# The second expert stage of a two-layer block: rows gathered and scattered by DMA in place of products on TensorE

## The chip, the cores and the metric

The kernel runs on one core of one Trainium2 chip. The metric is the device time of one execution in microseconds (us). A core has TensorE (PE, with its weight loads shown as PEld), VectorE (DVE), ScalarE (ACT), GpSimd (POOL) and SyncE (SP), which run side by side, each in its own order, and 16 DMA engines that all queues share.

## The reference

A two-layer block over 256 latent and 256 context tokens of 1024 numbers, in fp32. Each layer has a mixer and then a mixture of experts. The second layer's experts see only the 256 latent tokens:

```python
def moe(h, router_w, router_bias, w_gate, w_up, w_down):
    t = h.reshape(-1, D_MODEL)
    score = jax.nn.sigmoid((t @ router_w).astype(jnp.float32))
    ...
    _, idx = lax.top_k(masked, TOP_K)          # TOP_K = 2 of N_EXPERTS = 16
    w = jnp.take_along_axis(score, idx, -1)
    w = w / jnp.sum(w, -1, keepdims=True)
    combine = jnp.sum(jax.nn.one_hot(idx, N_EXPERTS, dtype=jnp.float32) * w[..., None], 1).astype(t.dtype)
    out = jnp.zeros_like(t)
    for e in range(N_EXPERTS):
        hid = jax.nn.silu(t @ w_gate[e]) * (t @ w_up[e])   # 1024 -> 512
        out = out + combine[:, e:e + 1] * (hid @ w_down[e])  # 512 -> 1024
    return out.reshape(shp)
```

## The kernel before

**Weights.** Each expert has 6.3 MB of weights: two tiles of 1 MB (128 x 2048) each for gate, up and down. `Feeder.load` issues them on SP into a ring of tiles named `raw` and `rawx` (RAWA = 3 and, in the second stage, RAWB1 = 4). A tile is used in two halves. `Feeder.one` turns a half into a pair of tiles `hl` or `hlx`: ACT copies it rounded to the short fp32 format (line 138), and DVE or POOL subtracts that from the source for the low part (line 140). This is a *split*; an expert needs 12. POOL takes every third where `feed.pool_lo` is 3 (line 1557), otherwise DVE takes all. A pair is free again when PE has used it; there are 4 pairs, and HLX_1 more in the second stage.

**First stage** (`moe`, 512 tokens). For each expert a list of up to 128 tokens is made by comparing positions (`slots`, line 1128). `gather` (line 1141) fetches their rows from XN in DRAM with an indirect DMA on POOL; `xT` (line 1157) turns them on PE and splits them into high and low. `expert` runs the gate product, half of the next expert's up product, the turn of the hidden tile, the other half, and the down product, with one split behind each block of products; every product is three matmuls (high by high, high by low, low by high). The result, times its weight, goes to YD in DRAM with an indirect DMA (line 1149). YD has a row for either of a token's two experts; at the end it is read back and summed. The last two experts don't go through DRAM: their rows are added by products with a 0/1 matrix (line 1349).

**Second stage** (`moe_latent`, 256 tokens). The experts are sorted by how many tokens they have; the places in BIG (0, 1, 4, 9) hold up to 128 tokens, the other twelve up to 64. Two small ones share an operand tile ("unit"), and high and low parts stand side by side in its 128 columns, so that a product has two matmuls of 512 columns instead of three (line 1553; 864 in all). Rows are not gathered. `collect` (line 1433) multiplies `xn`, which stays in SBUF, by the 0/1 matrix `PG` (line 1424), 16 matmuls in fp32 for each half of a unit's operand. A small expert's halves are added by products with `fold` (lines 1609, 1613). The result `y` is split into high and low (lines 1648, 1649) and added into four PSUM banks that are held through the stage: `combine`, eight matmuls an expert (line 1538) with the 0/1 matrix `PT` (line 1635).

`overflow` is a branch for the case that an expert has more tokens than its place holds; here it is not taken. In the second stage it stands ahead of the last expert, and all engines pass it.

What sets the order: inside `in_order()` every engine runs its instructions in the order in which the code issues them, so an instruction that waits holds up those behind it on its engine.

Of the kernel before, what the change touches and what calls it, by code (L numbers as in the profile page):

```python
# [56 lines left out]
HLX_1, AHEAD_1 = 4, 6  # L57
# [111 lines left out]
def _body(tc, nc, pool, psum, dram, a):  # L169
# [677 lines left out]
    def normed(layer, r, nh):  # L847
# [7 lines left out]
        for i in range(2):  # L855
            t = x_ = xn[:, D * i + 512 * nh:D * i + 512 * nh + 512]
            if layer:

                t = tmp()
                x_ = xn[:, D * i:D * i + D].rearrange("q (k p) -> q p k", k=8)[:, 64 * nh:64 * nh + 64]  # L860
            V.scalar_tensor_tensor(t, Hh(2 * r + i, nh), rs[:, 2 * r + i:2 * r + i + 1], psc, OP.mult, OP.mult)
            b_ = sh if engs[i] == "G" else psh
            if layer:
                t, b_ = (w.rearrange("q (p k) -> q p k", k=8) for w in (t, b_))
            XENG[engs[i]].tensor_tensor(x_, t, b_, OP.add)
# [111 lines left out]
    YD = dram.tile([1024, D], F32, name="YD")  # L977
    rank = pool.tile([128, 4, NE], F32, name="rank")
# [31 lines left out]
    def overflow(layer, nt, pl, pos, prepare=None, expert=None, finish=None):  # L1010
# [3 lines left out]
        with tc.If(rv > 128):  # L1014
            if layer:
# [3 lines left out]
                prepare(y)  # L1019
# [9 lines left out]
            with tc.For_i(0, NE, 1) as e:  # L1029
                re = nc.values_load(cnti[0:1, bass.ds(e, 1)], min_val=0, max_val=top)  # L1030
                we = expert(e) if expert else e
                for q in range(1, nt if layer == 0 else nt + 1):
                    with tc.If(re > 128 * q):
# [14 lines left out]
                        for k in range(8):  # L1048
                            T.transpose(b_[2 + k // 4][:, 128 * (k % 4):128 * (k % 4) + 128], xg[:, 128 * k:128 * k + 128] if layer else xg[:, k::8], ident)
# [20 lines left out]
                        for nh in range(2):  # L1070
                            V.tensor_scalar(y[:, 512 * nh:512 * nh + 512], b_[nh], odisp[:, 2:3], None, OP.mult)
                        G.indirect_dma_start(out=YD, out_offset=bass.IndirectOffsetOnAxis(ap=odispi[:, 0:1], axis=0),
                                             in_=y, in_offset=None, bounds_check=256 * nt - 1, oob_is_err=False)
            if finish:
                finish([wt, xh])

    def route(layer, nt):
# [36 lines left out]
        V.tensor_copy(RM[:, :n_, :, 0], rk)  # L1114
# [4 lines left out]
    def moe(layer, nt, pl, before_tail=None):  # L1119
# [82 lines left out]
        overflow(layer, nt, pl, posm)  # L1202
# [175 lines left out]
    def moe_latent(pl, xn):  # L1378
# [11 lines left out]
        units.sort()  # L1390
        iota2 = pl.tile([128, 128], F32, name="iota2")
# [5 lines left out]
        for j in range(NE):  # L1397
            G.memset(rcol[:, j:j + 1], float(at[j]))
        kc = pl.tile([128, NE], F32, name="kc")
# [3 lines left out]
        RMS = pl.tile([128, 2, NE, 2], F32, name="RMS")  # L1403
        toffs = pl.tile([128, 2], F32, name="toffs")
        for i in range(2):
            G.tensor_scalar(RMS[:, i, :, 0], pcol[:, 0:1].broadcast_to([128, NE]), 128.0 * i + 1.0, None, OP.add)
            G.memset(toffs[:, i:i + 1], -128.0 * i - 1.0)
        wd = pl.tile([128, NE, 2], F32, name="wd")
        dcol = pl.tile([128, NE, 2], F32, name="dcol")
# [4 lines left out]
        perm = pl.tile([128, NE, NE], F32, name="perm")  # L1414

        xsteps, se, sc, mk, rk = route(layer, nt)
        xsteps(2)
# [9 lines left out]

        def collect(unit, PG, k4):

            pt = bank()  # L1430
            for k in range(4):
                for i in range(2):
                    T.matmul(pt[:, 128 * k:128 * k + 128], xn[:, D * i + 128 * (4 * k4 + k):D * i + 128 * (4 * k4 + k) + 128],
                             PG[:, i, 0] if len(unit) == 1 else PG[:, i, :, 0:64], start=i == 0, stop=i == 1)
            return pt

        def split_operand(unit, pt, s, k4):
            if len(unit) == 1:
# [518 lines left out]
```

## Time and profile before

| | |
|---|---|
| median of 3 runs | 1244.71 us (1241.48 to 1245.55) |
| the profiled execution | 1236.13 us, span 1234.4 us |
| PE, DVE, ACT, POOL busy | 88%, 72%, 59%, 32% of the span |
| mean granted clock of TensorE | 0.961 |
| DMA | 308 MB, mean 250 GB/s |
| first stage, from first to last expert's first product | 303.4 to 606.9 us |
| second stage, the same | 856.4 to 1200.0 us |

Shares of the whole span mix mixers and expert stages. The two stages are to be read apart, each by its stretch of the trace. Busy time of an engine counts what overlaps once. Times in the trace count from the start of the span.

### The profile page before, as it was taken

How to read it: one execution, taken by the hardware profiler on the slowest of the kernel's cores; microseconds unless marked ns; L12 is line 12 of the kernel's file. 1: busy time of each engine (PE TensorE's matmuls, PEld its weight loads, DVE VectorE, ACT ScalarE, POOL GpSimd, SP SyncE). 2: the span in 40 equal slices, each digit the busy share in tenths (PEclk: the TensorE clock that was granted, in tenths of full speed). 3: DMA queues.
4: the chain of work that ended last, by engine and by line, in shares of the span. 5: the costliest groups of instructions: out<-in, count | busy, mean ns of one | idle time of the engine just before them, and what ended most of it. 6: DMA issues, size and time to landing. Idle time of an engine off the chain costs nothing. (4 is left out here: it accounts for less than half of the span.)

```text
span 1234.4 us, 15863 instructions
## 1 busy us (share of the span) xinstructions
PE 1091.7 (88%) x5595; PEld 812.2 (66%) x5596; DVE 884.6 (72%) x1118; ACT 724.8 (59%) x973; POOL 389.4 (32%) x396
## 2 busy tenths in 40 slices
PE   5889999994999999998779999996699898998883
PEld 3546454783777778777467766675577777777662
DVE  3444561747889998898974345857989889789983
ACT  3326642434878888887534234533667677677771
POOL 3150561623011111111434100122435554544551
PEclk9999999997999999999979999998899998998997
DMA  9763666904899999997963778352678787879840
GB/s 301 219 192 115 202 189 225 360 30 149 333 373 350 359 349 363 377 351 271 337 199 80 255 242 303 137 238 69 239 256 299 267 304 281 317 263 326 280 152 34
DMA packets 96529, 308.15 MB, mean 250 GB/s; under 512 B 16494, under 2 KB 57601, under 8 KB 67256
## 3 DMA queue, kind: packets, MB, share of 16 engines
q1 hardware_dynamic: 89576, 293.38, 67.2%
q0 software_dynamic: 6864, 13.66, 3.5%
q8 instruction: 47, 0.77, 0.3%
q14 instruction: 42, 0.34, 0.1%
HBM read 299.15 MB, written 11.60 MB: 252 GB/s over the span
## 5 line engine op out<-in xcount | busy, mean ns | idle before, releaser
L140 DVE TENSOR_TENSOR hl<-raw,hl 128x1024 fp32r<-128x1024 f32 x126 | 168.4, 1353 | 116.4 <-ACT hl L138 92.7
L140 DVE TENSOR_TENSOR hl<-rawx,hl 128x1024 fp32r<-128x1024 f32 x167 | 226.3, 1382 | 29.3 <-ACT hl L138 23.0
L138 ACT ACTIVATE hl<-raw 128x1024 fp32r<-128x1024 f32 x140 | 145.7, 1055 | 119.9 <-PE psa L456 40.6
L138 ACT ACTIVATE hl<-rawx 128x1024 fp32r<-128x1024 f32 x178 | 185.5, 1060 | 44.4 <-PE psb L1169 12.6
L1169 PE MATMUL psb<-hl,xT 128*128 128x512 f32 x696 | 172.1, 400 | 0.0
L1169 PEld LDWEIGHTS psb<-hl,xT 128*128 128x128 f32 x696 | 127.7, 188 | 27.4
L1553 PE MATMUL psa<-hl,xT 128*128 128x512 f32 x432 | 116.6, 417 | 15.8 <-DVE xT L1633 15.0
L1553 PE MATMUL psa<-hlx,xT 128*128 128x512 f32 x432 | 114.8, 412 | 16.0 <-DVE xT L1633 12.3
L1553 PEld LDWEIGHTS psa<-hl,xT 128*128 128x128 f32 x432 | 84.4, 200 | 39.4 <-DVE xT L1633 13.0
L1553 PEld LDWEIGHTS psa<-hlx,xT 128*128 128x128 f32 x432 | 83.0, 197 | 38.3 <-DVE xT L1633 11.2
L1266 PE MATMUL psa<-hl,xT 128*128 128x512 f32 x192 | 77.6, 404 | 3.7 <-DVE hl L140 1.7
L1266 PE MATMUL psb<-hl,xT 128*128 128x512 f32 x192 | 77.3, 403 | 0.1
L456 PE MATMUL psa<-nT,hl 128*128 128x512 f32 x264 | 69.6, 408 | 4.7 <-POOL nT L490 2.5
L456 PEld LDWEIGHTS psa<-nT,hl 128*128 128x128 f32 x264 | 48.6, 189 | 28.6 <-issue 6.9
L1141 POOL DMA_INDIRECT xg<-XN,dispi x16 | 21.5, 1341 | 141.9 <-PE psa L1251 68.7
L140 DVE TENSOR_TENSOR hlx<-rawx,hlx 128x1024 fp32r<-128x1024 f32 x38 | 60.2, 1594 | 3.7 <-ACT hlx L138 3.7
L456 PE MATMUL psb<-nT,hl 128*128 128x512 f32 x216 | 58.1, 415 | 4.8 <-DVE hl L140 2.6
L140 POOL TENSOR_TENSOR hlx<-rawx,hlx 128x1024 fp32r<-128x1024 f32 x18 | 48.3, 2686 | 42.4 <-ACT hlx L138 36.5
L140 POOL TENSOR_TENSOR hl<-rawx,hl 128x1024 fp32r<-128x1024 f32 x17 | 46.4, 2728 | 40.8 <-ACT hl L138 34.0
L138 ACT ACTIVATE hlx<-rawx 128x1024 fp32r<-128x1024 f32 x54 | 55.5, 1055 | 4.9 <-PE psa L1553 4.8
L140 POOL TENSOR_TENSOR hl<-raw,hl 128x1024 fp32r<-128x1024 f32 x14 | 38.3, 2738 | 60.6 <-ACT hl L138 54.7
L456 PEld LDWEIGHTS psb<-nT,hl 128*128 128x128 f32 x216 | 41.5, 196 | 20.0 <-issue 4.2
(504 smaller groups left out, 2146.9 us busy)
## 6 DMA issues: line engine op xcount, KB each, us to landing
rawx<-in_moe_w_up_dram SPq DMA_DIRECT2D x41, 1024.0 KB
rawx<-in_moe_w_gate_dram SPq DMA_DIRECT2D x40, 1024.0 KB
rawx<-in_moe_w_down_dram SPq DMA_DIRECT2D x37, 1024.0 KB
raw<-in_ada_w_dram SPq DMA_DIRECT2D x32, 1024.0 KB
raw<-in_moe_w_down_dram SPq DMA_DIRECT2D x25, 1024.0 KB
raw<-in_moe_w_gate_dram SPq DMA_DIRECT2D x21, 1024.0 KB
raw<-in_moe_w_up_dram SPq DMA_DIRECT2D x20, 1024.0 KB
rawx<-in_ada_w_dram SPq DMA_DIRECT2D x16, 1024.0 KB
```

The costliest lines, as they stand in the source:

```text
L138: nc.scalar.activation(h3, src, AF.Copy, scale=1.0 if self.gate is None else self.gate)
L140: (nc.gpsimd if self.pool_lo and self.ns % self.pool_lo == 0 else nc.vector).tensor_tensor(l3, src, h3.bitcast(F32), OP.subtract)
L456: ins = T.matmul(pt, l, r, start=k == 0 and m == 0, stop=k == 7 and m == 2)
L1141: G.indirect_dma_start(out=xgs[e % 2], out_offset=None, in_=XN, in_offset=bass.IndirectOffsetOnAxis(ap=dispi[:, e, 1:2], axis=0), bounds_c ...
L1169: ins = T.matmul(out_, l, r_, start=m == 0, stop=m == last)
L1266: T.matmul(pb, l, w_[:, 512 * nh:512 * nh + 512], start=m == 0, stop=m == 11)
L1553: ins = T.matmul(po, l, w_[:, c0:c0 + 512], start=k == 0 and m == 0, stop=k == n * per - 1 and m == len(mm) - 1)
```

## The change

The second stage gets the first's ways and order. `gather` fetches a unit's rows from XN with an indirect DMA, `tokens` turns and splits them; `scatter` writes an expert's rows to a new DRAM tensor YL, 1024 rows of 1024 numbers: four for each token, two for either of its experts. A small expert writes both, from the high and the low columns of its tile; a big one writes the first alone, and the second rows are zeroed in the mixer. YL is read back ahead of the last expert and summed on POOL and DVE. `expert` has one split behind each block. All splits run on DVE (`pool_lo` stays 0). HLX_1 goes from 4 to 2.

```diff
-HLX_1, AHEAD_1 = 4, 6
+HLX_1, AHEAD_1 = 2, 6
...
-                x_ = xn[:, D * i:D * i + D].rearrange("q (k p) -> q p k", k=8)[:, 64 * nh:64 * nh + 64]
...
-        if nh and layer == 0:
+        if nh:
             for i in range(2):
                 Q.dma_start(XN[128 * (2 * r + i):128 * (2 * r + i) + 128], xn[:, D * i:D * i + D])
...
+    YL = dram.tile([1024, D], F32, name="YL")
...
-            PG = pl.tile([128, 512], F32, name="PG", tag="PG", bufs=2)[:, :256 * n].rearrange("p (i k s) -> p i k s", i=2, k=n)
+            PG = pl.tile([128, 512], BF, name="PG", tag="PG", bufs=3)[:, :256 * n].rearrange("p (i k s) -> p i k s", i=2, k=n)
...
+        def gather(n):
+            unit, PG = units[n], PGs[n]
+            pd = bank()
+            w = 128 // len(unit)
+            for c in range(len(unit)):
                 for i in range(2):
+                    for x_ in (2, 3):
+                        T.matmul(pd[w * c:w * c + w, 0:1], PG[:, i, c, :w], RM[:, i, unit[0], x_:x_ + 1],
+                                 start=i == 0 and x_ == 2, stop=i == 1 and x_ == 3)
+            V.tensor_scalar(gidx[:, n:n + 1], pd[:, 0:1], 4096.0, None, OP.add)
+            G.indirect_dma_start(out=xgs[n % 2], out_offset=None, in_=XN,
+                                 in_offset=bass.IndirectOffsetOnAxis(ap=gidx[:, n:n + 1], axis=0),
+                                 bounds_check=128 * nt - 1, oob_is_err=False)
+            return pd
...
+        def info(j):
...
+            for o, cols in ((0, (0, 1)), (2, (4, 5, 6))) + (((1, (2, 3)),) if j >= NE - 2 else ()):
+                for i in range(2):
+                    for x_ in cols:
+                        T.matmul(pd[:, o:o + 1], PGs[n][:, i, c], RM[:, i, j, x_:x_ + 1], start=i == 0 and x_ == cols[0],
+                                 stop=i == 1 and x_ == cols[-1])
...
+        def scatter(j, y):
+            G.indirect_dma_start(out=YL, out_offset=bass.IndirectOffsetOnAxis(ap=dispi[:, j, 0:1], axis=0),
+                                 in_=y, in_offset=None, bounds_check=1023, oob_is_err=False)
...
+        def tokens(n):
...
+            for k4 in range(2):
+                pt = bank()
+                for k in range(4):
+                    T.transpose(pt[:, 128 * k:128 * k + 128], xgs[n % 2][:, 4 * k4 + k::8], ident)
...
+                S.activation(hi, src, AF.Copy)
+                V.tensor_tensor(lo, src, hi.bitcast(F32), OP.subtract)
...
-        feed.pool_lo, feed.boost, feed.ahead = PL_1, 0, 1
+        feed.boost, feed.ahead = BOOST, 1
...
+        def expert(j, us):
...
+            if j < NE - 2:
+                info(j)
+            pg = bank()
+            for b in range(4):
+                ins = block(j, [pg], b)
+                if b < 3:
+                    split()
+                    rest(1)
...
+            split()
+            if new is not None and new > 1:
+                gather(new)
...
+            if j + 1 < NE:
+                pu = bank()
+                for b in (0, 1):
+                    block(j + 1, [pu], b)
+                    split()
             ph = bank()
+            if two:
+                for o, w_ in ((256, us), (0, gs)):
+                    for k in range(4):
+                        T.matmul(ph[:, o + 64 * k:o + 64 * k + 64], w_[:, k::4], fold, start=True, stop=True)
                 sl_, hd = tmp(256), tmp(256)
                 S.activation(sl_, ph[:, :256], AF.Silu)
                 V.tensor_tensor(hd, sl_, ph[:, 256:], OP.mult)
...
+            if j + 1 < NE:
+                for b in (2, 3):
+                    block(j + 1, [pu], b)
+                    split()
...
+            pd = [bank(), bank()]
+            for b in range(4):
+                block(j, pd, b)
+                if b < 3:
+                    split()
+                    rest(2)
+            rest(99)
+            w_ = disp[:, j, 2:3]
+            if j < NE - 2:
+                y = pl.tile([128, D], F32, name="y", tag="y", bufs=3)
+                for nh in range(2):
+                    S.activation(y[:, 512 * nh:512 * nh + 512], pd[nh], AF.Copy, scale=w_)
+                scatter(j, y)
...
+            split()
+            if new is not None and new > 1:
+                tokens(new)
+            return pu
...
+        yss = [[feed.raw_tile(True) for _ in range(2)] for _ in range(nt)]
+        for i in range(nt):
+            for h in range(2):
+                Q.dma_start(yss[i][h].rearrange("p (q d) -> p q d", q=2),
+                            YL[512 * i:512 * i + 512].rearrange("(p h q) d -> p h q d", h=2, q=2)[:, h])
+        def add(i, st):
+            y0, y1 = yss[i]
+            if st == 0:
+                G.tensor_tensor(y1[:, :D], y1[:, :D], y1[:, D:], OP.add)
+            elif st == 1:
+                V.tensor_tensor(y0[:, :D], y0[:, :D], y0[:, D:], OP.add)
+            elif st == 2:
+                V.tensor_tensor(y0[:, :D], y0[:, :D], y1[:, :D], OP.add)
+            elif st == 3:
+                V.tensor_tensor(y0[:, :D], y0[:, :D], gb, OP.mult)
+            else:
+                V.tensor_tensor(Hi(i), Hi(i), y0[:, :D], OP.add)
         with in_order():
+            for i in range(nt):
+                add(i, 0)
+            for i in range(nt):
+                for st in range(1, 5):
+                    later.append(lambda i=i, st=st: add(i, st))
+            expert(NE - 1, us)
...
+    nil = tmp()
+    G.memset(nil, 0.0)
+    low_rows = YL.rearrange("(p r q) d -> p r q d", r=4, q=2)[:, :, 1]
+    for nh in range(2):
+        G.dma_start(low_rows[:, :, 512 * nh:512 * nh + 512], nil.unsqueeze(1).broadcast_to([128, 4, 512]))
```

The order on PE from the start of one small expert into its down product, before (lines of the kernel before):

```order
L1433 MATMUL psa<-PG,xn 128x128 x16
L1452 MATMUL psa<-RMS,PG 128x2 x4
L1553 MATMUL psa<-hl,xT 128x512 x8
L1553 MATMUL psa<-hlx,xT 128x512 x8
L1609 MATMUL psa<-fold,tmp 128x64 x4
L1538 MATMUL psb<-y,PT 128x512 x8
L1613 MATMUL psa<-fold,tmp 128x64 x4
L1553 MATMUL psa<-hlx,xT 128x512 x8
```

Behind the change (lines of the changed kernel: 1471 `tokens`, 1451 `info`, 1566 `block`, 1616 `fold`; the ten matmuls of `info` are cut to one):

```order
L1471 MATMUL psb<-ident,xg 128x128 x4
L1471 MATMUL psa<-ident,xg 128x128 x4
L1451 LDWEIGHTS PG
L1451 MATMUL psb<-RM,PG 128x1
...
L1566 MATMUL psa<-hl,xT 128x512 x8
L1566 MATMUL psa<-hlx,xT 128x512 x8
L1566 MATMUL psb<-hl,xT 128x512 x8
L1616 MATMUL psa<-fold,tmp 128x64 x8
L1566 MATMUL psb<-hl,xT 128x512 x8
L1566 MATMUL psb<-hlx,xT 128x512
L1566 MATMUL psa<-hlx,xT 128x512
```

The 16 fp32 products on `xn` became four transposes, and the eight products on `y` between the foldings (1538) are gone; in their place stands the first half of the next expert's up product.

DVE in a small expert that prepares the next unit, before:

```order
L140 TENSOR_TENSOR hl<-rawx,hl 128x1024
L1446 TENSOR_TENSOR xT<-psa,xT 128x4x2x64
L140 TENSOR_TENSOR hl<-rawx,hl 128x1024
L1446 TENSOR_TENSOR xT<-psa,xT 128x4x2x64
L140 TENSOR_TENSOR hl<-rawx,hl 128x1024
L140 TENSOR_TENSOR hlx<-rawx,hlx 128x1024
L1616 TENSOR_TENSOR tmp<-tmp,psa 128x256
L140 TENSOR_TENSOR hlx<-raw,hlx 128x1024
L1633 TENSOR_TENSOR xT<-tmp,xT 128x4x64
L1635 TENSOR_TENSOR PT<-iota,dcol 128x256
L140 TENSOR_TENSOR hlx<-raw,hlx 128x1024
L140 TENSOR_TENSOR hl<-raw,hl 128x1024 x2
```

Behind the change (1480 `tokens`, 1454 and 1456 `info`, 1619 and 1627 the hidden tile):

```order
L140 TENSOR_TENSOR hl<-rawx,hl 128x1024 x2
L140 TENSOR_TENSOR hl<-raw,hl 128x1024 x2
L140 TENSOR_TENSOR hlx<-raw,hlx 128x1024 x2
L1480 TENSOR_TENSOR xT<-psa,xT 128x4x2x64
L1480 TENSOR_TENSOR xT<-psb,xT 128x4x2x64
L1454 COPY disp<-psa 128x1
L1456 TENSOR_SCALAR dispi<-psa,base 128x1
L140 TENSOR_TENSOR hl<-raw,hl 128x1024 x2
L140 TENSOR_TENSOR hl<-rawx,hl 128x1024 x2
L140 TENSOR_TENSOR hlx<-rawx,hlx 128x1024 x2
L1619 TENSOR_TENSOR tmp<-tmp,psb 128x256
L1627 TENSOR_TENSOR xT<-tmp,xT 128x4x64
```

PT and the low half of `y` (1635, 1649) are gone, and the third splits, which stood on POOL, stand here.

DVE in the last expert, behind the branch, before:

```order
L140 TENSOR_TENSOR hl<-raw,hl 128x1024 x2
L1616 TENSOR_TENSOR tmp<-tmp,psa 128x256
L1633 TENSOR_TENSOR xT<-tmp,xT 128x4x64
L1635 TENSOR_TENSOR PT<-iota,dcol 128x256
L1649 SCALAR_TENSOR_TENSOR y<-psa,wd,y 128x512 x2
L1671 TENSOR_TENSOR tmp<-psb,raw 128x512 x3
L1672 TENSOR_TENSOR H<-H,tmp 128x512
L1671 TENSOR_TENSOR tmp<-psb,raw 128x512
L1672 TENSOR_TENSOR H<-H,tmp 128x512
```

Behind the change (1693 to 1699 are the steps of `add`):

```order
L140 TENSOR_TENSOR hl<-raw,hl 128x1024 x3
L1693 TENSOR_TENSOR rawx<-rawx 128x1024
L140 TENSOR_TENSOR hl<-raw,hl 128x1024
L1695 TENSOR_TENSOR rawx<-rawx 128x1024
L1697 TENSOR_TENSOR rawx<-rawx,gf 128x1024
L1619 TENSOR_TENSOR tmp<-tmp,psa 128x256
L1627 TENSOR_TENSOR xT<-tmp,xT 128x4x64
L1699 TENSOR_TENSOR H<-H,rawx 128x1024
L1693 TENSOR_TENSOR raw<-raw 128x1024
L1695 TENSOR_TENSOR raw<-raw 128x1024
L1697 TENSOR_TENSOR raw<-raw,gf 128x1024
L1699 TENSOR_TENSOR H<-H,raw 128x1024
```

Four splits instead of two and eight operations on rows of YL have come in, three of them ahead of the product of the hidden tile (1619), five behind its low part (1627).

## Rows read from the trace of the kernel before

**Rows 1.** The page's slices: 40 equal parts of the span.

```profile
DMA  9763666904899999997963778352678787879840
GB/s 301 219 192 115 202 189 225 360 30 149 333 373 350 359 349 363 377 351 271 337 199 80 255 242 303 137 238 69 239 256 299 267 304 281 317 263 326 280 152 34
```

**Rows 2.** Busy time by stretch: a part of the first stage, of the second.

```profile
core 0: us, PE busy (x) PEld busy (x) DVE busy (x) ACT busy (x) POOL busy (x), PEclk, DMA share, GB/s
330.00:570.00 240.00, 232.68 (x1110) 186.19 (x1109) 216.20 (x254) 196.20 (x228) 31.16 (x27) 1.00 0.96 357
880.00:1180.00 300.00, 267.32 (x1342) 219.74 (x1343) 264.73 (x235) 217.48 (x260) 149.31 (x56) 0.96 0.83 291
```

**Rows 3.** Timeline of the second stage: start, duration, engine, line, tiles, count.

```profile
849.56 0.19 DVE L1116 TENSOR_TENSOR posm<-mask,psb 128x32 f32<-128x32 f32 x1
...
856.40 3.05 PE L1553 MATMUL psa<-hl,xT 128*128 128x512 f32 x12
...
887.24 5.66 PE L1553 MATMUL psa<-hlx,xT 128*128 128x512 f32 x24
...
895.53 3.73 PE L1433 MATMUL psa<-PG,xn 128*128 128x128 f32 x32
...
1199.99 2.11 PE L1553 MATMUL psa<-hl,xT 128*128 128x512 f32 x8 [0.50 <-DVEq L1014]
...
1208.01 0.42 DVE L1616 TENSOR_TENSOR tmp<-tmp,psa 128x256 f32<-128x256 f32 x1 [4.42 <-ACT tmp L1615]
...
1208.91 0.43 DVE L1633 TENSOR_TENSOR xT<-tmp,xT 128x256 fp32r<-128x256 f32 x1 [0.48 <-ACT xT L1632]
...
1215.53 1.41 DVE L1649 SCALAR_TENSOR_TENSOR y<-psa,wd,y 128x512 fp32r<-128x512 f32 x2 [5.86 <-ACT y L1648]
```

**Rows 4.** Timeline of the first stage, its start and its end.

```profile
293.15 0.21 DVE L1116 TENSOR_TENSOR posm<-mask,psa 128x64 f32<-128x64 f32 x1
...
303.41 6.92 PE L1169 MATMUL psa<-hl,xT 128*128 128x512 f32 x24
...
585.23 0.80 SPq L1312 DMA_DIRECT2D raw<-YD  x2
...
590.14 6.08 POOL L1322 TENSOR_TENSOR raw<-raw 128x1024 f32<-128x1024 f32 x2 [7.19 <-DMA raw<-YD]
...
610.64 1.22 DVE L1324 TENSOR_TENSOR raw<-raw,gb 128x1024 f32<-128x1024 f32 x1
```

**Rows 5.** First stage, 330 to 570: line 1169, line 140, one group.

```profile
330.00:570.00 240.00, 151.90 (x614) 112.76 (x615) 1.00 0.96 357
...
330.00:570.00 240.00, 177.18 (x150) 0.00 (x0) 1.00 0.96 357
...
L1128 DVE TENSOR_TENSOR pm<-iota,posm 128x512 bf16<-128x512 f32 x13 | 8.9, 682 | 0.0
```

**Rows 6.** Second stage, 880 to 1200: lines 1553 and 140, groups.

```profile
880.00:1200.00 320.00, 201.81 (x785) 151.64 (x785) 0.96 0.79 277
...
880.00:1200.00 320.00, 193.76 (x118) 160.07 (x59) 0.96 0.79 277
...
L1553 PE MATMUL psa<-hl,xT 128*128 128x512 f32 x393 | 106.0, 417 | 15.5 <-DVE xT L1633 15.0 <-DVEq L1014 0.5
...
L1649 DVE SCALAR_TENSOR_TENSOR y<-psa,wd,y 128x512 fp32r<-128x512 f32 x30 | 21.0, 738 | 4.8 <-ACT y L1648 4.8
...
L1635 DVE TENSOR_TENSOR PT<-iota,dcol 128x256 fp32r<-128x256 f32 x15 | 19.8, 1322 | 0.0
...
L1424 DVE TENSOR_TENSOR PG<-iota,posS 128x512 f32<-128x512 f32 x6 | 15.1, 2525 | 0.0
```

**Rows 7.** Busy time in the mixer, as the zero rows come.

```profile
660.00:670.00 10.00, 10.00 (x59) 7.69 (x60) 4.02 (x10) 4.37 (x8) 6.71 (x11) 1.00 0.04 9
```

**Rows 8.** Gathers of the first stage: PE's wait for them, landing times.

```profile
PEld psb L1157 <- DMA xg<-XN,dispi: 10.7, 8, 2.5
...
DMA to landing us min/median/max: 4.7/7.5/10.0
```

More of the change, by code (lines that the diff above doesn't have):

```diff
@@ L1398, in moe_latent @@
             G.memset(rcol[:, j:j + 1], float(at[j]))
+        room = pl.tile([128, NE], F32, name="room")
+        for j in range(NE):
+            G.memset(room[:, j:j + 1], 128.0 - cap[j])
         kc = pl.tile([128, NE], F32, name="kc")
@@ L1460, in moe_latent, with split @@
+        def split(n=1):
+            for _ in range(n):
+                feed.one()
+        for t in xgs:
+            S.activation(t, score[:, 0, 0:1].broadcast_to([128, D]), AF.Copy, scale=0.0)
         PGs = [places(unit, posm) for unit in units[:2]]
-        V.tensor_scalar(one, PGs[0][:, 0, 0, 0:1], 0.0, 1.0, OP.mult, OP.add)
-        s = operand()
-        for k4 in range(2):
-            split_operand(units[0], collect(units[0], PGs[0], k4), s, k4)
+        for n in range(2):
+            pd = gather(n)
@@ L1465, in moe_latent @@
+        V.tensor_scalar(one, pd[:, 0:1], 0.0, 1.0, OP.mult, OP.add)
         feed.gate, feed.boost = one, GBOOST
@@ L1557, in moe_latent, with rest @@
-        feed.pool_lo, feed.boost, feed.ahead = PL_1, 0, 1
-        unit_of = {j: (n, c) for n, unit in enumerate(units) for c, j in enumerate(unit)}
-        ops = [s]
+        feed.boost, feed.ahead = BOOST, 1
+        later, last, zeros = deque(), [], []
+        def rest(n):
+            for _ in range(n):
+                if later:
+                    later.popleft()()
         def parts_of(j):
@@ L1660, in moe_latent @@
+            split()
+            if new is not None and new > 1:
+                tokens(new)
+            return pu
+        with in_order():
+            tokens(0)
+            us = bank()
+            for b in range(4):
+                block(0, [us], b)
+                split()
+            tokens(1)
+            for j in range(NE - 1):
+                us = expert(j, us)
+            split(2)
+            gb, fg = (pl.tile([128, D], F32, name="gf", tag="xg", bufs=2) for _ in range(2))
             G.dma_start(fg, a["final_g"].unsqueeze(0).broadcast_to([128, D]))
@@ L1670, in moe_latent @@
+        for i in range(nt):
+            for nh in range(2):
+                po = bank()
+                m = 0
+                for PT, yy in zip(PTs, last):
+                    for q in range(2):
+                        T.matmul(po, PT[:, 128 * i:128 * i + 128], yy[q][:, 512 * nh:512 * nh + 512], start=m == 0, stop=m == 3)
+                        m += 1
                 t = tmp()
-                V.tensor_tensor(t, acc[i][nh], gb[:, 512 * nh:512 * nh + 512], OP.mult)
+                V.tensor_tensor(t, po, gb[:, 512 * nh:512 * nh + 512], OP.mult)
```

274 lines of the change are left out of this document (102 added, 172 removed).

## The prediction

> **What bounds the kernel now.** I read the page's slices first [rows 1]. The change leaves the first expert stage alone and rebuilds the second in its image, so both stages have to be read: the first fills slices 11 to 20 of the 40, the second 28 to 40. In the first the slices reach 333 to 377 GB/s; in the second 239 to 326. The stretches give the same in one line each [rows 2]: the first stage moves 357 GB/s at a DMA share of 0.96, the second 291 at 0.83, with PE at 267 of 300 us, DVE at 265 and POOL at 149, where POOL had 31 of 240 us in the first. So the second stage is not held by transfers.
>
> Its pace is read from the timeline [rows 3]. The first product of the stage starts at 856.40, the first product of the last expert (behind the branch) at 1199.99. Between them lie one "up" product (24 matmuls, 5.7 us by the row that starts at 887.24) and 15 experts: (343.6 − 5.7) / 15 = 22.5 us an expert. In the first stage an expert has 48 matmuls of line 1169; 614 of them in 240 us are 12.8 experts, 18.76 us each [rows 5]. That although a first-stage expert has 72 long matmuls, and the second stage's 864 over 16 experts make 54.
>
> The groups of the second stage say why. There 118 splits on DVE take 193.8 us, 1.64 each, and 59 on POOL 160.1, 2.7 each [rows 6]; in the first stage all are on DVE at 177.2 / 150 = 1.18 [rows 5]. Two on DVE (3.3 us) beside one on POOL (2.7) are three in 3.3 us; DVE alone would do three in 3.5. POOL's third of the work bought almost nothing. By the same rows PG takes 2.5 us there and PT 1.3. PE stands idle mostly until DVE has written an operand (line 1633: 15.0 us ahead of one half of the products, in rows 6).
>
> **The change part by part**, first per expert in the window 880 to 1200, whose 785 long matmuls [rows 6] are 785 / 54 = 14.5 experts.
>
> DVE, splits: all 177 run on DVE, at 1.18: 209, or +15. The price holds if POOL is what stretched them; were it something else, 177 x 1.64 = 290 (+97) is the upper bound. I take 1.18, because the same shape has it beside 357 GB/s in the first stage.
>
> DVE, the rest: the low half of y goes for all but two experts (28 of 30 at 0.70 us, −19.6); PT goes (−19.8); PG becomes bf16, as pm is in the first stage at 0.682 (8 x (2.53 − 0.68) = −15) [rows 5, 6]. The small index copies cost what those of wd and dcol cost. Sum −39 of 282 us busy (265 per 300): 243 / 14.5 = 16.8 us an expert.
>
> PE: collecting goes (256 matmuls in the window, 32 in 3.73 us, 0.117 each: 30 us), and adding the products (112 x 0.236, from 24 in 5.66: 26 us) [rows 3]. Eight transposes per operand (64) and ten matmuls of one column an expert (145) come; priced as collecting ones, 24 us. What is left is 785 x 0.236 + 24 and folding, which has 176 small matmuls, 21 us by the same price: 230, or 15.9 an expert.
>
> DMA: six tiles of 1.049 MB are 6.29 MB an expert. 256 tokens with two experts each give 512 rows of 4 KB gathered and up to 1024 scattered (a small expert writes two for a token, from the high and the low columns), 0.39 MB an expert at most. 6.68 MB at 357 GB/s is 18.7 us.
>
> So DMA (18.7) comes ahead of DVE (16.8) and PE (15.9). For the pace I take **18.8**, the first stage's own 18.76: it carried 335 GB/s of weights with the same order of work and with 1024 rows gathered and 1024 scattered, and all three were nearly full there (rows 2). Lower bound 16.8 (DVE alone); upper bound 20.5, if the wait chain in a small expert (fold, silu, product, two copies) shows: in rows 3 it ends in the last expert with the two DVE rows at 1208.01 and 1208.91, 1.3 us from the start of one to the end of the other, and only two products of 0.94 us hide it. Saved: 15 x (22.5 − 18.8) = 55.5 us.
>
> Start of the stage: the first operand now comes through a gather. In the first stage posm starts at 293.15 and the first product at 303.41, 10.3 us [rows 4]; in the second now 849.56 and 856.40, 6.8 [rows 3]. +3.4; between 0 and +7, if rows of XN are written late.
>
> End: 4 MB are read back where nothing was. SP issues them behind its last weights and behind the branch, so they land around the start of the last expert. In the first stage four such reads are issued from 585.23, and POOL's first sum starts at 590.14, 4.9 us later; two sums on POOL take 6.1 us [rows 4]. Two POOL sums and eight DVE operations of the splits' size (9.8 us at 1.22, rows 4) enter the last expert; in the DVE order three stand ahead of the hidden product and five ahead of the last y. DVE has gaps there (4.42 and 5.86 us before the rows at 1208.01 and 1215.53, rows 3), which take most of it. The last two experts' products are still added on PE (16 matmuls where 8 were). +4, between 0 and +10.
>
> Costed at nothing: the zero rows written in the mixer (2.1 MB, 6 us at 357 GB/s; in 660 to 670 DMA moves 9 GB/s [rows 7], and if the bias rows that are read there had to wait behind them, it would be those 6 us), the POOL queue (16 scatters and 10 gathers in place of 64 splits; the first stage's POOL, with 16 of each, is busy 31 of 240 us [rows 2]) and xn written straight.
>
> Sum: −55.5 + 3.4 + 4 = −48 us on the span of 1234.4, so 1186. The profiled execution took 1236.13 and is 8.6 below the median of the runs, 1244.71; I put the change on the median: 1244.7 − 48, about **1196**.
>
> On the gathers a page speaks against the change. In the first stage they land in 4.7 to 10.0 us, median 7.5, with DVE busy 216 of 240 us, and PE waited for them 10.7 us in 13 experts [rows 2, 8]. The Trainium skill, "SBUF — State Buffer", section "Who interferes with whom", says that a DMA issued from GpSimd stalls when VectorE keeps it from writing descriptors. By the rows that costs under 1 us an expert and is inside 18.76; by the rule a busier DVE would make the operand late, which is in the next case.
>
> **The rivals.** *The chain shows (20.5 us an expert).* Experts with 48 products are shorter than the first stage's 72, so gather, transposes and fold have less to hide behind. For it: the 15.0 us in which PE waits for line 1633 ahead of half of its products [rows 6]. Against: DVE has 16.8 of work and PE 15.9, so the chain has 2 to 3 us of slack. 15 x 2.0 = 30 saved, minus 7.4: 1222.
>
> *DVE alone (16.8).* DMA would have to give 6.68 / 16.8 = 398 GB/s; the best slice shows 377 [rows 1]. 15 x 5.7 = 86, minus 7.4: 1167. The Trainium skill, "HBM Reference", section "Specifications (TRN2)", gives a core that streams alone about 425 GB/s; no run here shows it.
>
> *Slower: the second stage's transfers can't go faster.* They differ from the first's: addresses come from registers, and 7 tiles are in flight (RAWA + RAWB1) where the first stage had up to 11. If the 291 GB/s are a ceiling and not a result, an expert takes 6.68 / 0.291 = 23.0 us, 15 x 0.5 are lost, and start and end stay: 1244.7 + 7.5 + 7.4 = 1260. It decides below 6.68 / (22.5 − 7.4 / 15) = 303 GB/s. For it: no slice of the stage reaches the first's rate. Against: 291 at a share of 0.83 would be 350 at 1.0, and one slice shows 326.
>
> *The order does not come out as in the first stage.* The orders on PE and DVE show that it does; I give it nothing.
>
> **How the numbers follow.** First case 0.62 (own range 1180 to 1212), the chain 0.18, DVE alone 0.06, slower 0.14. A measurement tells 0.3% here, 3.7 us. A pace of 22.0 ± 0.25 would be "same"; I give it 0.03, taken from the slower case (0.02) and the chain (0.01). Faster 0.62 + 0.17 + 0.06 = 0.85, same 0.03, slower 0.12. The range leaves out the slower case and most of DVE alone: 1174 to 1228.
>
> **What will show it.** In the changed profile: splits on DVE at 1.2 us throughout and POOL near a tenth; the second stage at 340 GB/s or more and a share over 0.93; 18 to 19.5 us an expert; PE idle before the products of small experts under 2 us each; first product about 10 us behind posm; from the branch to the end of the span 38 us instead of 34.4. It is wrong if splits stay at 1.6 us with POOL idle, if the share stays near 0.83 with PE waiting for gathers or for the chain, or if the last expert stands more than 10 us for YL.

## The result and the profile after

The changed kernel takes 1206.93 us (median of 4 runs, 1206.42 to 1208.97) against 1244.41 (4 runs) for the kernel before: a ratio of 0.9705, with a 95% interval from 0.9685 to 0.9726. The forecast was 1196, its range 1174 to 1228. The profiled execution after lies at the median (1206.66, span 1205.0); that of before was 8 us below its own. So the spans differ by 29.4 us where the times differ by 37.5.

The page's slices of the changed kernel, which answer to [rows 1]:

```profile
DMA  9763757912899999999765757835279999999960
GB/s 299 232 195 90 216 166 253 355 70 83 329 353 365 356 353 367 358 346 354 294 198 190 214 205 253 301 130 209 86 252 361 363 370 373 358 363 354 351 249 35
```

The second stage now reaches 351 to 373 GB/s, as the first does. A stretch of it, as in [rows 2] (busy us of PE, PEld, DVE, ACT, POOL, each with its count; then clock, DMA share, GB/s), all engines first, then the splits of line 140 alone:

```profile
880.00:1140.00 260.00, 249.15 (x1235) 200.05 (x1235) 223.57 (x262) 206.89 (x261) 38.71 (x23) 0.95 0.95 354
880.00:1140.00 260.00, 193.38 (x166) 0.95 0.95 354
```

The share is 0.95, POOL is busy 39 of 260 us, a split takes 193.38 / 166 = 1.17 us, where [rows 6] had 1.64 on DVE and 2.7 on POOL. The marks of the stage in the timeline, which answer to [rows 3]:

```profile
861.02 0.19 DVE L1109 TENSOR_TENSOR posm<-mask,psb 128x32 f32<-128x32 f32 x1
867.72 1.22 PE L1566 MATMUL psb<-hlx,xT 128*128 128x512 f32 x2
874.85 4.21 PE L1566 MATMUL psb<-hlx,xT 128*128 128x512 f32 x10 [5.91 <-DVE xT L1480]
...
1160.93 2.10 PE L1566 MATMUL psb<-hl,xT 128*128 128x512 f32 x8 [0.45 <-PEq L1008]
1164.71 3.74 PE L1616 MATMUL psa<-fold,tmp 128*128 128x64 f32 x16
```

From the first product (867.72) to the first of the last expert (1160.93) the stage takes 293.2 us where it took 343.6: (293.2 − 5.7) / 15 = 19.2 us an expert, 50.4 us less. The first product comes 11.3 us later than before, and from the last expert to the span's end it is 44.1 us where it was 34.4. −50.4 + 11.3 + 9.7 = −29.4.

Two of these losses show in the trace. In the mixer, where [rows 7] had an empty DMA, the zero rows lie around the bias rows on POOL's queue:

```profile
667.23 0.81 POOL L1812 DMA_DIRECT2D YL<-tmp  x1
667.94 0.63 POOL L1788 DMA_DIRECT2D RP<-tmp  x1
669.07 0.74 POOL L1812 DMA_DIRECT2D YL<-tmp  x1
...
679.91 1.46 PE L353 MATMUL psb<-raw,condT 128*32 128x512 f32 x8 [3.76 <-DMA raw<-in_ada_w_dram]
680.78 2.92 POOL L1803 TENSOR_TENSOR Gb<-Gb,tmp 128x384 f32<-128x384 f32 x3 [10.97 <-DMA Gb<-RP]
```

The bias sums wait 11 us for their rows. And in the last expert the sums of the rows read back (L1693 to L1697) stand on DVE ahead of the hidden product (L1619):

```profile
1166.63 1.22 DVE L1693 TENSOR_TENSOR rawx<-rawx 128x1024 f32<-128x1024 f32 x1
...
1171.22 1.23 DVE L1695 TENSOR_TENSOR rawx<-rawx 128x1024 f32<-128x1024 f32 x1 [2.23 <-POOL rawx L1691]
1172.48 1.23 DVE L1697 TENSOR_TENSOR rawx<-rawx,gf 128x1024 f32<-128x1024 f32 x1
1173.62 0.42 DVE L1619 TENSOR_TENSOR tmp<-tmp,psa 128x256 f32<-128x256 f32 x1
1173.95 2.43 DVE L1714 TENSOR_SCALAR tmp<-iota,dcol 128x128 fp32r<-128x128 f32 x3
1176.30 0.41 DVE L1627 TENSOR_TENSOR xT<-tmp,xT 128x256 fp32r<-128x256 f32 x1
...
1176.77 0.79 PE L1566 MATMUL psb<-hl,xT 128*128 128x512 f32 x1 [8.32 <-DVE xT L1627]
```

The same wait in the kernel before:

```profile
1209.39 3.08 PE L1553 MATMUL psa<-hlx,xT 128*128 128x512 f32 x8 [1.90 <-DVE xT L1633]
```

Behind the hidden product stand three of four compares (L1714) which the order shown with the change leaves out: they make PT for the last two experts, and the low part of the hidden tile (L1627) waits for them. PE's wait ahead of the down product is 8.3 us where it was 1.9, and the 16 products that add the last two experts take 4.1 us where eight took 2.2: together 8.3 of the 9.7 us.

### The profile page after: what moved, and what is told of

It reads as the page before. It is cut to its first block, busy times and chain, and to the rows that moved or that the text cites. A ratio compares the mean times of both kernels' runs of the same rounds, so it can differ in the third digit from the quotient of the medians.

```text
span 1205.0 us, 15507 instructions
## 1 busy us (share of the span) xinstructions
PE 1074.6 (89%) x5411; PEld 791.8 (66%) x5412; DVE 848.9 (70%) x1168; ACT 712.1 (59%) x971; POOL 274.8 (23%) x365
## 5 line engine op out<-in xcount | busy, mean ns | idle before, releaser
L140 DVE TENSOR_TENSOR hl<-raw,hl 128x1024 fp32r<-128x1024 f32 x156 | 187.0, 1229 | 122.3 <-ACT hl L138 99.1
L140 DVE TENSOR_TENSOR hl<-rawx,hl 128x1024 fp32r<-128x1024 f32 x202 | 248.4, 1270 | 30.1 <-ACT hl L138 25.7
L138 ACT ACTIVATE hl<-rawx 128x1024 fp32r<-128x1024 f32 x196 | 202.4, 1059 | 40.9 <-PE psb L1162 13.9
L1162 PE MATMUL psb<-hl,xT 128*128 128x512 f32 x696 | 173.1, 402 | 0.0
L1162 PEld LDWEIGHTS psb<-hl,xT 128*128 128x128 f32 x696 | 128.5, 190 | 27.6
L1566 PE MATMUL psb<-hl,xT 128*128 128x512 f32 x304 | 97.8, 430 | 9.7 <-DVE xT L1627 8.3
L1566 PE MATMUL psa<-hl,xT 128*128 128x512 f32 x268 | 88.3, 433 | 0.9 <-DVE hl L140 0.9
L1259 PE MATMUL psa<-hl,xT 128*128 128x512 f32 x192 | 77.1, 402 | 2.0 <-DVE hl L140 1.4
L1259 PE MATMUL psb<-hl,xT 128*128 128x512 f32 x192 | 77.0, 401 | 0.1
L1566 PEld LDWEIGHTS psb<-hl,xT 128*128 128x128 f32 x304 | 59.9, 204 | 26.0 <-DVE xT L1627 8.5
L1566 PEld LDWEIGHTS psa<-hl,xT 128*128 128x128 f32 x268 | 53.5, 207 | 14.4 <-DVE hl L140 3.1
L1566 PE MATMUL psb<-hlx,xT 128*128 128x512 f32 x152 | 51.2, 417 | 6.9 <-DVE xT L1480 5.9
L140 DVE TENSOR_TENSOR hlx<-rawx,hlx 128x1024 fp32r<-128x1024 f32 x38 | 45.6, 1221 | 10.1 <-ACT hlx L138 10.1
L622 POOL DMA_DIRECT2D cz<-ups x64 | 34.9, 550 | 57.5 <-DVE th L689 42.1
L1566 PE MATMUL psa<-hlx,xT 128*128 128x512 f32 x140 | 46.6, 402 | 1.2 <-DVE hlx L140 0.8
```

The costliest lines, as they stand in the source:

```text
L138: nc.scalar.activation(h3, src, AF.Copy, scale=1.0 if self.gate is None else self.gate)
L140: (nc.gpsimd if self.pool_lo and self.ns % self.pool_lo == 0 else nc.vector).tensor_tensor(l3, src, h3.bitcast(F32), OP.subtract)
L622: G.dma_start(z[32 * j:32 * j + 32, G4, :, :284], ups_[g][32 * G4:32 * G4 + 32, :, j:j + 284])
L1162: ins = T.matmul(out_, l, r_, start=m == 0, stop=m == last)
L1259: T.matmul(pb, l, w_[:, 512 * nh:512 * nh + 512], start=m == 0, stop=m == 11)
L1566: ins = T.matmul(po, l, w_[:, c0:c0 + 512], start=k == 0 and m == 0, stop=k == 4 * per - 1 and m == len(mm) - 1)
```

## The experiments

Twelve more kernels ran on three chips, each beside the kernel before (1239 to 1242 us there), so they are compared by their ratio to it. The variants of the changed kernel in experiments 1, 2, 3, 6 and 12 can't be told from it by their intervals; there the stretches of the traces decide, one trace for each kernel. "Mixer" is the time from the first product of the second layer's mixer to its first latent projection, "to router" from there to the router's first count, "stage" and "end" as above, in us.

| kernel | ratio, 95% interval | mixer | to router | stage | end |
|---|---|---|---|---|---|
| before | 1 | 23.7 | 163.1 | 343.6 | 34.4 |
| before, splits on DVE alone | 0.9669, 0.9626–0.9712 | 23.7 | 163.1 | 302.8 | 34.5 |
| before, every 6th split on POOL | 0.9862, 0.9825–0.9899 | 23.7 | 163.1 | 326.4 | 37.3 |
| before, HLX_1 = 2 | 1.0251, 1.0206–1.0296 | 23.6 | 168.7 | 367.7 | 34.4 |
| before, DVE alone, HLX_1 = 2 | 0.9991, 0.9969–1.0013 | 23.7 | 169.6 | 340.9 | 34.3 |
| before, zero rows written | 1.0017, 0.9986–1.0047 | 29.2 | 161.9 | 340.9 | 37.3 |
| changed | 0.9705, 0.9685–0.9726 | 30.2 | 167.0 | 293.2 | 44.1 |
| changed, every 3rd split on POOL | 1.0138, 1.0076–1.0200 | 29.6 | 167.6 | 343.3 | 45.4 |
| changed, zero rows early | 0.9780, 0.9712–0.9848 | 23.7 | 167.6 | 298.8 | 44.4 |
| changed, zero rows late | 0.9731, 0.9682–0.9781 | 23.7 | 167.8 | 296.4 | 44.0 |
| changed, fold in a row | 0.9771, 0.9710–0.9832 | 30.5 | 166.9 | 295.8 | 44.6 |
| changed, sums behind | 0.9759, 0.9676–0.9843 | 29.4 | 167.7 | 294.8 | 45.4 |
| changed, the last three together | 0.9717, 0.9679–0.9754 | 23.7 | 167.0 | 296.2 | 45.6 |
| changed, no low halves of weights | 0.9394, 0.9351–0.9438 | 29.3 | 167.6 | 246.2 | 47.5 |

**1. Zero rows moved to the end of the first expert stage.** The five lines that write YL move up in the code, ahead of the first ada_w loads of the layer:

```diff
     close_pool(cmY)
     feed.extra2 = None
+    nil = tmp()
+    G.memset(nil, 0.0)
+    low_rows = YL.rearrange("(p r q) d -> p r q d", r=4, q=2)[:, :, 1]
+    for nh in range(2):
+        G.dma_start(low_rows[:, :, 512 * nh:512 * nh + 512], nil.unsqueeze(1).broadcast_to([128, 4, 512]))
     feed.only = True
```

> The zero rows are written where the first expert stage has just ended (620 to 630 us, where DMA moves 74 GB/s) instead of beside the bias rows of the mixer. Theory, zero rows hold up the mixer's loads: the product that waits 3.8 us for the second ada_w tile and the bias additions that wait 11 us go back to the times of before, the second stage's first product comes at 857 to 862 us instead of 867.7, and the time falls from 1206.9 to 1196-1201. Rival, the mixer is late for other reasons (other pools, other order): first product at 866 to 868, time 1205-1208.

The mixer's start falls from 30.2 to 23.7 us, the length of before. But the writes were issued at 642 us, not near 625, beside the loads for the mixer, and in this trace the mixer's first product came some 8 us later against the end of the first stage (64.5 us behind the last expert's first product, 56.0 and 57.5 in experiments 2 and 3). Half the theory holds: the 6.5 us are the zero rows'; that the 8 us are theirs too fits, and is not shown.

**2. Fold over columns in a row.**

```diff
-            S.activation(t, pb, AF.Copy)
+            S.activation(t.rearrange("q (k p) -> q p k", k=4), pb.rearrange("q (p k) -> q p k", k=4), AF.Copy)
...
-                        T.matmul(ph[:, o + 64 * k:o + 64 * k + 64], w_[:, k::4], fold, start=True, stop=True)
+                        T.matmul(ph[:, o + 64 * k:o + 64 * k + 64], w_[:, 128 * k:128 * k + 128], fold, start=True, stop=True)
```

> ACT writes the kept gate and up products with the four column groups apart, and the fold reads 128 columns in a row instead of every fourth. Theory, the fold's strided reads (16 matmuls in 3.7 us instead of 2.0) are on the path of the small experts: 12 x 1.7 = 20 us of PE go, the pace falls from 19.2 to 18.7 us or less, time 1197-1200. Rival, transfers set the pace and PE only waits elsewhere: the fold takes 2 us and the time stays within 2 us of 1206.9.

The fold's matmuls of 880 to 1140 us fall from 37.4 us (160) to 17.7 (151), yet the stage takes 295.8 us. PE's 20 us were not on the path, as the rival says; whether transfers set the pace is answered by experiment 11.

**3. The sums behind the hidden product.**

```diff
                 ins = block(j, [pg], b)
                 if b < 3:
                     split()
-                    rest(1)
...
                 block(j, pd, b)
                 if b < 3:
                     split()
-                    rest(2)
-            rest(99)
+                    rest(1)
...
             split()
+            rest(99)
             if new is not None and new > 1:
                 tokens(new)
```

> In the last expert no sum of the rows read back stands ahead of the hidden product on DVE; three stand among the down products and the other five behind the last y. Theory, those three put 6 us into PE's wait of 8.3 us: that wait falls under 3 us and the time from 1206.9 to 1201-1204. Rival, DVE has the same work to do in the tail (8 sums of 1.22 us) and is late at the very end instead: PE's wait falls, the time stays within 1.5 us.

PE's wait falls from 8.3 to 3.3 us, and the end takes 45.4 us. The rival holds: the same sums are then late behind the last product. The end follows DVE's added work in either order; no run takes that work away. The three compares still stand between the hidden product and its low part (2.1 us here).

**4. The zero rows alone**, added to the kernel before where the changed one has them: behind `position_bias()` the five lines of experiment 1, with a YL that nobody reads.

> The kernel before with the two zero-row writes of 1 MB each added in the mixer, and nothing else; nobody reads these rows. Theory, they hold up the mixer's loads by themselves: the second stage's first product 6 to 11 us later, time 1244.4 -> 1250-1255. Rival, the delay in the changed kernel comes from its other pools and order: time within 2 us of 1244.4.

The mixer's start goes from 23.7 to 29.2 us, with the same row as in the changed kernel ([10.56 <-DMA Gb<-RP] before the bias sums). But the time moves by 0.17%, inside the interval, and in this trace the stretches from there to the last expert are some 4 us shorter (161.9 for 163.1 and 340.9 for 343.6). The place is shown; that its 5.5 us reach the end is not.

**5. Fewer split tiles alone.**

```diff
-HLX_1, AHEAD_1 = 4, 6
+HLX_1, AHEAD_1 = 2, 6
```

> The kernel before with HLX_1 = 2 in place of 4 (two pairs of extra split tiles instead of four in the second stage) and nothing else. The stretch from the mixer's first latent projection to the router's first count took 163 us in the kernel before and 167 in the changed one and in its variants. Theory, the fewer split tiles alone move the first expert's splits ahead of the last attention turns on ACT and DVE: 166 to 168 us here, time 2 to 6 us up. Rival, these 4 us belong to the other parts of the change: 163 us, time as before.

The mixer's end takes 168.7 us, near the 167.0 of the changed kernel: this constant moves some of the first experts' splits forward (four at 791 to 798 us, where the kernel before has none between 782 and 808). The size was missed by far: the time goes up 2.5%, 31 us, and most of it is the stage (367.7).

**6. Zero rows in an empty stretch.** `nil` is made from POOL's last sum, so that the writes start at 833.6 us; the two writes follow as in experiment 1.

```diff
     for _ in out_proj(gb, mhl, 2, 1, False):
         pass
+    nil = pg.tile([128, 512], F32, name="nil")
+    G.tensor_scalar(nil, Hh(1, 1), 0.0, None, OP.mult)
...
```

> The zero rows are written behind POOL's last sum of the first half of the output projection, near 836 us, where DMA moves nothing for 20 us, instead of beside the bias rows. Theory, the 6.5 us in the mixer's start were the zero rows' and nothing else is late for them: 24 us instead of 30 from the mixer's first product to its first latent projection, 163 or 167 us from there to the router as with the other variants, time 5 to 8 us below the changed kernel (1199-1202 against 1206.9, or as much against what the changed kernel takes on this chip). Rival, the rows of XN or the first gather now wait behind them: first gather later by 3 us or more, no gain.

The mixer's start is back at 23.7 us and the router no later than in the other variants: the theory holds for the place. The first gather is issued 1.5 us behind posm, as in the changed kernel, so that part of the rival does not hold. But the time (1205.85, ratio 0.9731) can't be told from the changed kernel's, and the stage is 3 us longer in this trace (296.4).

**7. All splits on DVE, nothing else**, in the kernel before.

```diff
-        feed.pool_lo, feed.boost, feed.ahead = PL_1, 0, 1
+        feed.pool_lo, feed.boost, feed.ahead = 0, 0, 1
```

> The kernel before with all splits of the second stage on DVE, none on POOL; collecting and adding products stay. Theory, POOL's third bought almost nothing, because it stretched DVE's splits from 1.2 to 1.6 us: splits at 1.2 us, DVE at 280 of 300 us, pace 21 to 22.5 us an expert, time 1222 to 1245. Rival, POOL's splits were the whole loss: pace under 20 us, time under 1210, and gather and scatter give nothing. Rival the other way, DVE alone can't carry it: pace over 23, time over 1250.

1199.02 us against 1238.89: with collecting, adding products, fp32 PG and all, this one constant gives 40 us, as much as the whole change, at (302.8 − 5.7) / 15 = 19.8 us an expert. By pace and time the first rival holds. DVE groups of it from 880 to 1160 us (busy us, mean ns of one, idle before it):

```profile
L140 DVE TENSOR_TENSOR hl<-rawx,hl 128x1024 fp32r<-128x1024 f32 x52 | 61.8, 1218 | 3.3 <-ACT hl L138 3.3
...
L1635 DVE TENSOR_TENSOR PT<-iota,dcol 128x256 fp32r<-128x256 f32 x15 | 6.2, 416 | 0.0
...
L1633 DVE TENSOR_TENSOR xT<-tmp,xT 128x256 fp32r<-128x256 f32 x11 | 4.6, 417 | 0.0
...
L1424 DVE TENSOR_TENSOR PG<-iota,posS 128x512 f32<-128x512 f32 x6 | 4.1, 682 | 0.0
...
L1649 DVE SCALAR_TENSOR_TENSOR y<-psa,wd,y 128x512 fp32r<-128x512 f32 x29 | 20.4, 743 | 0.9 <-ACT y L1648 0.9
L1446 DVE TENSOR_TENSOR xT<-psa,xT 128x512 fp32r<-128x512 f32 x16 | 10.9, 683 | 0.0
```

In [rows 6] the same PG took 2525 ns and PT 1322. Not the type of the output made them slow but POOL's splits beside them. The last two rows show where that ends: with one input in PSUM (`psa`), L1649 takes 743 ns here and 738 in [rows 6], and L1446, in the kernel before from 880 to 1200 us, the same 682:

```profile
L1446 DVE TENSOR_TENSOR xT<-psa,xT 128x512 fp32r<-128x512 f32 x16 | 10.9, 682 | 0.0
```

The rows above that were stretched in the kernel before have both inputs in SBUF.

The longest of what PE waited for from 880 to 1140 us (us, times, longest), of before and then of this kernel:

```profile
PE psa L1553 <- DVE xT L1633: 17.8, 10, 3.5
PE psa L1627 <- DVE tmp L1622: 7.8, 1, 7.8
PE psa L1433 <- DVE PG L1424: 3.8, 5, 1.1
```

```profile
PE psa L1553 <- DVE xT L1633: 3.7, 5, 1.1
```

**8. POOL's splits put back into the changed kernel.**

```diff
-        feed.boost, feed.ahead = BOOST, 1
+        feed.pool_lo, feed.boost, feed.ahead = PL_1, BOOST, 1
```

> The changed kernel with every third split of the second stage on POOL, as before. Theory, POOL's splits stretch DVE's to 1.5-1.7 us and its gathers and scatters are issued behind them: pace 19.2 -> 20.5 to 22 us, time 15 to 40 us up. Rival, transfers hold the pace at 19 us whatever engine splits: within 4 us of the changed kernel.

1259.33 us, 1.4% above the kernel before and 4.5% above the changed one by the ratios, more than the theory had. The stage (343.3) is as long as before the change, 22.5 us an expert. The splits of line 140 from 880 to 1140 us (busy us of DVE, of POOL):

```profile
880.00:1140.00 260.00, 183.81 (x96) 130.46 (x49) 0.92 0.85 305
```

183.81 / 96 = 1.91 us each on DVE, where 1.17 stood. That it is slower than before is not the gathers' doing: the old collecting with POOL's splits and as few tiles stands at 1.0251 (experiment 5), 1.1% above this one.

**9. The changed kernel's engines and tiles with the old collecting.** HLX_1 = 2 and `pool_lo` = 0 in the kernel before (edits 5 and 7 together).

> The kernel before with all splits of the second stage on DVE and HLX_1 = 2: the changed kernel's engines and tiles, with collecting and adding products kept. Together with the kernel that has HLX_1 = 4 (1199 us) and the changed one (1207) it prices the tiles and the gathers apart. Theory, fewer tiles cost much where a split is late, that is beside POOL (32 us), and less on DVE alone: 1207 to 1218, so the gathers by themselves give 0 to 10 us. Rival, tiles cost the same 32 us here: 1225 to 1235, and the gathers give 20 to 30.

1239.07 us, 0.9991: both the theory and its rival were too low. At four pairs the old collecting stands at 0.9669, at two at 0.9991: the tiles cost 3.3%, 40 us. At equal engines and tiles the changed order stands at 0.9705 against 0.9991: gathers and the new order are worth 2.9%, some 35 us. Both prices belong to their partner: the tiles were priced in the old order alone, the gathers at two pairs alone. What the missing tiles do is seen in ACT's waits from 880 to 1140 us, here and then with four pairs:

```profile
ACT hl L138 <- PE psa L1553: 53.8, 33, 5.5
```

```profile
ACT hl L138 <- PE psa L1553: 8.9, 9, 3.6
```

ACT can't write the next high half until PE has read a tile out. Here the splits come in bursts of two and three between whole products; the changed code puts one split behind each quarter of a product, and in its trace ACT's writes of `hl` wait for PE not at all in that stretch. This fits tiles that are read out and refilled evenly, but gathering and the new order were not run apart. Nor was the old order's head start changed: it splits AHEAD_1 = 6 halves ahead of its first expert, as many as there are pairs with HLX_1 = 2; the changed code does not use that constant. With a smaller one the tiles could cost less, which no run shows.

**10. A half dose.** PL_1 = 6 in place of 3 in the kernel before.

> The kernel before with every sixth split of the second stage on POOL instead of every third. Theory, POOL's splits stretch whatever DVE does beside them, in proportion to POOL's busy time: about half of the 40 us come back, 1213 to 1225, mean split on DVE about 1.35 us, POOL's still 2.7. Rival, a small share on POOL is the best of both: at or under 1199.

1222.98 us: of the 3.3% that leaving POOL gives, 1.4% come with half the dose. DVE's splits take 188.37 / 126 = 1.50 us and POOL's 75.22 / 25 = 3.0, both more than expected; the theory holds for the time, and a small share on POOL is not better than none.

**11. No low halves.**

```diff
-                mm = [(parts[0], hi), (parts[0], lo)] + [(x_, hi) for x_ in parts[1:]]
+                mm = [(parts[0], hi)]
```

and `Feeder.one` leaves out the subtraction in this stage. For the four big experts the new line also drops the low part of the tokens, so that of 864 products 480 go: 384 that read low halves of weights and 96 that don't.

> The changed kernel without the low halves of the weights in the second stage: neither DVE's splits nor the products that read them; loads, gathers, scatters and the rest stay. Theory, transfers hold the changed stage's pace (DMA share 0.95, 354 GB/s): 18 to 19 us an expert as they stand, the stage 5 to 15 us shorter, no more. Rival, DVE and PE hold it: the stage falls by 40 us or more, and DMA goes well over 370 GB/s.

1166.17 us. From the first product to the issue of the reads of YL the stage takes 250.6 us where the changed kernel took 291.3. The page's slices, and the stretch 900 to 1110:

```profile
GB/s 297 221 208 114 224 157 215 356 148 73 240 339 322 365 345 349 356 352 371 343 269 179 180 237 223 251 294 135 217 50 394 419 420 420 418 415 408 414 238 37
```

```profile
900.00:1110.00 210.00, 175.38 (x754) 129.60 (x755) 29.78 (x85) 195.34 (x247) 22.04 (x22) 0.74 1.01 416
```

416 GB/s, with the same loads, gathers and scatters. The rival holds: 354 at a share of 0.95 was no ceiling. Over 880 to 1140 us the share is 0.95 here too, at 389 GB/s. In the changed kernel the loads themselves waited (SP, 880 to 1140 us):

```profile
SPq L112 <- DVE hl L140: 127.3, 46, 5.4
SPq L112 <- DVE hlx L140: 58.8, 26, 3.9
```

A load is issued when DVE has split the tile it goes into; without DVE's halves it is issued earlier. Could DVE's work hold transfers up in another way, without these waits? Two stretches of the kernel before speak against it (all engines, as in [rows 2]): one moved 423 GB/s, the other 397 with DVE busy 8.45 of 10 us.

```profile
820.00:826.00 6.00, 6.00 (x27) 4.85 (x26) 1.88 (x3) 0.00 (x0) 2.46 (x2) 1.00 1.03 423
340.00:350.00 10.00, 8.31 (x36) 6.38 (x34) 8.45 (x8) 7.95 (x10) 1.62 (x2) 1.00 1.00 397
```

**12. The three side costs taken back together** (edits 2, 3 and 6).

> The changed kernel with its three side costs taken back together: zero rows near 836 us, fold over 128 columns in a row, sums of the rows read back behind the last expert's hidden product. Theory, 6 us from the zero rows, 0 to 3 from the fold, 0 to 2 from the end: 1197 to 1201, level with the kernel before with its splits on DVE (1199), not better. Rival, fold and sums add more when the zero rows are out of the way: 1190 or less.

1204.83 us (0.9717): missed by 4 us. Only the zero rows' 6.5 us show in the trace; the stage (296.2) and the end (45.6) don't get shorter. The kernel before with its splits on DVE, at 0.9669, stays the fastest that computes the whole: by its interval level with the changed kernel or a little better, and it differs from before in one constant.

## Why the prediction was right, and where not

**The sum.** Forecast −48 us on the span, measured −29.4: the pace gave 50.4 of 55.5, the start cost 11.3 where 3.4 was put, the end 9.7 where 4 was. The start is outside its own bounds (0 to 7), the other two are inside. The span fell 19 us short of the forecast, the time (37.5) only 11: the profile of before was 8 us under its median, the changed kernel's was not, and the working put the change on the median. That this helped is luck.

**Pace.** 19.2 us came out near 18.8, which was read from the first stage [rows 5], and share, GB/s and split time came as the last part said (POOL had 15% where near a tenth was put). The reason beside it failed: "So DMA (18.7) comes ahead of DVE (16.8) and PE (15.9)". Transfers were not the limit (experiment 11: 416 GB/s). DVE's term was right: 223.57 us busy in 260 / 19.2 = 13.5 experts are 16.5. PE's was not: 249.15 / 13.5 = 18.4, of which folding has 2.8 where 176 matmuls at 0.117 us gave 1.4; the changed code reads the fold's weights at a stride. But taking that back (experiment 2) made nothing faster. Of DVE's splits and PE's products, which experiment 11 takes away together, it stays open which one holds the 19.2.

**What the pace came from.** This is the step that failed although its sum fits. The working saw splits stretched by POOL, then let DVE's other savings come from taking PT away and from a bf16 PG. Experiment 7 keeps both and has them at 416 and 682 ns. The engine change alone is worth 40 us. Against it stands a line of the diff that the working never priced: HLX_1 from 4 to 2, 40 us in the old order (experiment 9; 31 beside POOL, experiment 5). Gathers with the new order, at two pairs, give 35 us back. In the stage alone the steps are 343.6, 302.8, 340.9 and 293.2 us: −41 + 38 − 48 is near the forecast's −55.5. These are three terms of this size, of which one was not in the sum and one was credited to other edits; that they came out near it is luck.

"POOL's third of the work bought almost nothing" was too mild: 3.3 us for three splits against 3.5 counts the splits alone, and POOL stretched DVE's other work with two inputs in SBUF beside them. The Trainium skill, "SBUF — State Buffer", section "Who interferes with whom", has the rule: a DVE instruction with two SBUF inputs contends with a GpSimd instruction that reads SBUF, for the port pair that the two engines share. The traces agree: PG takes 682 ns with POOL idle and 2525 beside it, while L1649 and L1446, with one input in PSUM, are not stretched (experiment 7). By that rule the splits, PT and PG of [rows 6] would have been suspect, and L1649 not.

**Start.** "Costed at nothing: the zero rows" failed, at 6.5 us; its own alternative (6 us if the bias rows must wait) was the right size (experiments 4 and 6). That is the delay in its place; no run shows a shorter time without it. Four more come from the mixer's end (167.0 for 163.1), where HLX_1 alone makes as much (experiment 5: 168.7), and one from ahead of the mixer. The gather itself made the first product no later (6.7 us behind posm, not 10), but the second ten wait 5.9 us for their operand; that is in the stage.

**End.** "DVE has gaps there, which take most of it" is the step that was mis-sized: the end grew by 9.7 us, the size of the added DVE work (eight sums of 1.22 us; the compares of line 1714, 2.7 us, were not counted). In the changed order it comes out as PE's wait of 8.3 us; where that was taken down to 3.3 (experiment 3), it came out behind the last product, and the end stayed. That DVE's work is the cause is argued from this, and not shown by a run without it.

**Rivals.** The ceiling of 291 GB/s did not come; DVE alone would have needed 398 GB/s, and experiment 11 shows that transfers would have carried it. There the Trainium skill, "HBM Reference", section "Specifications (TRN2)", agrees with the run: 425 GB/s for a core alone, 416 measured. "The best slice shows 377" was a reading of 31 us slices: the trace of before already has 423 GB/s in 820 to 826 us and 397 in 340 to 350. (The first stage's "333 to 377" also leaves out slice 19, 271.) PE's waits for a small expert's operand (line 1627) are 1.4 us in 880 to 1140; the chain doesn't show. The gathers landed later than in the first stage (median 9.4 us where 7.5 stood), but PE's waits for them are 4.1 and 2.6 us there (line 1471), half a microsecond an expert. That a part of the change could cancel another was no rival, and should have been.

## What to carry to other kernels

Before a change that mixes several edits is priced, run or price its smallest one alone: here one constant did as much as the rewrite. Where a like instruction has different means in two stretches of one profile (1.18 and 1.64, 0.68 and 2.5 us), look for who works beside it before anything else. Price tiles given up for new buffers like time, by what waits for them; and don't read a DMA share of 0.95 as a ceiling as long as the loads wait to be issued: here it stood beside 354 and 389 GB/s.

## What the runs showed of the hardware

Splits on POOL beside DVE cost more than they carry, at every dose tried: 126.5 us of POOL's work in 260 us made DVE's 94 splits 1.65 us long (kernel before, 880 to 1140 us), and at half the share they still took 1.50 (experiment 10), against 1.17 without POOL (experiment 7: 193.23 / 165). Instructions of DVE with one input in PSUM kept their time beside POOL's splits (738 and 743 ns, 682 and 683). The one core's transfers reached 416 GB/s over 210 us (experiment 11). The weights of a matmul read from every fourth fp32 column load in 327 ns instead of 191 (PEld of the fold, changed kernel and experiment 2), and the matmul follows: 37.38 / 160 = 0.23 us each against 17.67 / 151 = 0.12.
